# Second feed-forward of a diffusion layer: pools that wait tile by tile, block sums taken from the split parts, and the first output projection moved between the products of one block

## The chip, the cores and the metric

One core of a Trainium2 chip runs the whole program. The metric is device time in microseconds (us) of one execution. A core has a matrix engine (TensorE, PE in the profile; its weight loads are PEld), VectorE (DVE), ScalarE (ACT), GpSimd (POOL) and SyncE (SP), which here issues nearly all DMAs. [...]

## The reference, cut to what matters

One layer works on 512 latent tokens and 256 context tokens of width 1024. It has a first SwiGLU feed-forward, a mixer, and a second SwiGLU feed-forward on the 512 latent tokens. The change touches the second one alone.

```python
def swiglu(y, w_in, w_out):                 # y: 512 x 1024, w_in: 1024 x 5632, w_out: 2816 x 1024
    a, b = jnp.split(y @ w_in, 2, axis=-1)
    return (jax.nn.silu(a) * b) @ w_out
x = ada_out(x, swiglu(ada_in(x, mod, 2, norm_pre[l, 2]), ffn_w_in[l, 1], ffn_w_out[l, 1]), mod, 2, norm_post[l, 2], 0.5)
```

All of it is float32.

## The kernel before

**Precision by splitting.** Every float32 operand of a large product is split into a high part (a copy into a format that TensorE reads in one pass, made by ACT in `split_hi`, L81) and a low part (source minus high, made by DVE in `split_lo` through `sub_to`, L78). `mm3` (L97 to L99) then makes one product out of three matmuls: high by high, low by high, high by low. `mm3p` (L102) is the same with its order fixed. `split_w` splits a weight tile of 128x1024.

**The second feed-forward** works through 22 blocks f of 128 hidden columns. For f = 0 and 1 it makes the a and b products with the full 2 x 24 matmuls per 256 tokens (`products`, `block`), then `gate` takes silu(a) * b and splits it into gh and gl. For f = 2 to 21 it uses a fast form, `in_fast`: the 512 tokens and the 1024 inputs are cut into 2 x 2 blocks (y11, y12, y21, y22), the two weight tiles too (x11, x12 in `ra`, x21, x22 in `rb`), and by Winograd's scheme seven products (12 matmuls of 256 columns each) stand in for eight. This needs sums of blocks. On the side of the tokens `combine` makes t1 = y12 - y11, t2 = y22 - t1, t3 = y22 - y12 and t4 = y21 - t2 once, each split into parts (its second half, t3 and t4, is the function `rest`). On the side of the weights each f makes s1 = x21 + x22 and s2 = s1 - x11 (tile `s12`), s3 = x11 - x21 and s4 = x12 - s2 (tile `s34`), splits both, and splits x11, x12 (tile x) and x22.

In `combine`, y is first put together again from its stored parts yh and yl (four DVE operations of 128x1024, L295, into the tile `yr`); the differences and the low parts follow.

**Output projection.** The f's go in pairs. After the two blocks of pair i, `out_g` multiplies pair i-1 by its rows of w_out: 4 token tiles x 2 column halves, each 2 x 3 matmuls of 512 columns into a bank `pz`, then DVE copies (pair 0, L410) or adds (the others, L412) the bank to the tile z. `out_g` loads and splits its two w_out tiles itself (L395, tag `wo`).

**Order.** The program is written in one order, but the build re-orders it: for each engine it lays out the instruction that is earliest in the program among those that its own estimate takes as ready, and a tile is only given a buffer when one of its tag is free. L97 to L99 may thus move among each other's products; L102 and other marked instructions stay in place. The second feed-forward starts like this (L1187 to L1221): while the last token tiles go through the mixer's output norm, the products of f = 0 and f = 1 for the first 256 tokens (`f2ps[0]`, `f2ps[1]`) and of f = 0 for the last 256 (`f2ps[2]`) are made in order. Then the mixer's pool `mix` closes and the pool `ffn2` opens on its memory.

```python
        for p in f2ps[:2]:
            f2.gate(*p)
        rest = f2.combine(256)
        f2.gate(*f2ps[2])
        f2.block(1, *b1)
        rest()
        f2.fast = True
        f2.run(lambda f: ((NCTX, NLAT),), started=(0, 1))
```

**Buffers that matter.** `raw`: 5 tiles for loaded weights. `win`: 8 tiles for split weights. `sw` (weight sums s12, s34, and t1, t2 of `combine`, the tile `tf`): 2 tiles. `pa`: 4 banks and `pz`: 2 banks for products. A pool opened on memory that another pool had waits, as a whole, for the last instruction that used that other pool. `mix` holds, at its start, the tile `wx` (half of the weights of f = 0), behind it 16 tiles `h`, and then small ones.

Of the kernel before, what the change touches and what calls it, by code (L numbers as in the profile page):

```python
# [8 lines left out]
F32 = mybir.dt.float32  # L9
F32R = mybir.dt.float32r  # L10
# [33 lines left out]
def tile_layer(ctx: ExitStack, tc: tile.TileContext, x, c, ctxt, c_ctx, w_mod, b_mod, norm_pre, norm_post,  # L44
# [194 lines left out]
    class Ffn:  # L239
        def __init__(self, wi, wo_ap, tiles, c_lo, c_hi):  # L240
            self.wi, self.wo_ap, self.tiles, self.c_lo = wi, wo_ap, tiles, c_lo
            self.ncol = c_hi - c_lo
            self.g, self.w, self.fast = {}, {}, False

        def scope(self, pool, done, filler, junk):
            self.pool, self.done, self.filler, self.junk = pool, done, filler, junk
# [37 lines left out]
        def block(self, f, c0, n):  # L284
            self.gate(f, c0, n, self.products(f, c0, n))

        def combine(self, n):


            self.n, c1, c2 = n, self.c_lo, self.c_lo + n  # L290
            k1, k2, cs1, cs2 = slice(0, 4), slice(4, 8), slice(c1, c1 + n), slice(c2, c2 + n)
            y = self.pool.tile([P, KD, 2 * n], F32, tag="z", name="yr", bufs=1)
            for k in (k1, k2):
                for i, cs in enumerate((cs1, cs2)):
                    V.tensor_tensor(out=y[:, k, i * n:(i + 1) * n], in0=yh[:, k, cs].bitcast(F32),  # L295
                                    in1=yl[:, k, cs].bitcast(F32), op=ALU.add)
            y11, y12, y21, y22 = (y[:, k, i * n:(i + 1) * n] for k in (k1, k2) for i in range(2))

            def full():
                return self.pool.tile([P, 4, n], F32, tag="sw", name="tf", bufs=2)  # L300

            t1, t2 = full(), full()
            sub_to(V, t1, y12, y11)
            sub_to(V, t2, y22, t1)
            part_of = iter(self.room(n))

            def split(src):
                hi, lo = next(part_of)
                split_hi(src, hi)
                split_lo(src, hi, lo)  # L310
                return hi, lo

            t2s, t1s = split(t2), split(t1)

            def rest():
                sub_to(V, y12, y22, y12)
                sub_to(V, y21, y21, t2)
                t3s, t4s = split(y12), split(y21)
                own = [(yh[:, k, cs], yl[:, k, cs]) for k, cs in ((k1, cs1), (k2, cs1), (k2, cs2))]
                self.moving = dict(y11=own[0], y21=own[1], y22=own[2], t1=t1s, t2=t2s, t3=t3s, t4=t4s)  # L320

            return rest

        def in_fast(self, f):

            n, pool = self.n, self.pool
            ra, rb = self.loads(f)
            x11, x12, x21, x22 = ra[:, 0:512], ra[:, 512:1024], rb[:, 0:512], rb[:, 512:1024]
            s12, s34 = (pool.tile([P, D], F32, tag="sw", name="sw", bufs=2) for _ in range(2))
            s1, s2, s3, s4 = s12[:, 0:512], s12[:, 512:1024], s34[:, 0:512], s34[:, 512:1024]  # L330
            xh, xl = split_w(ra)
            V.tensor_add(s1, x21, x22)
            sub_to(V, s2, s1, x11)
            sh, sl = split_w(s12)
            sub_to(V, s3, x11, x21)
            sub_to(V, s4, x12, s2)
            uh, ul = split_w(s34)
            x22p = part()
            split_hi(x22, x22p[:, 0:512])
            split_lo(x22, x22p[:, 0:512], x22p[:, 512:1024])  # L340
            lo, hi = slice(0, 512), slice(512, 1024)

            def product(q, wh, wl, y, first=True):
                wh, wl, (mh, ml) = kc(wh), kc(wl), self.moving[y]
                for k in range(4):
                    mm3(q[:, 0:n], wh[:, k], wl[:, k], mh[:, k], ml[:, k], first and k == 0, k == 3,
                        skip_group_check=not first)

            def temp(name):
                return pool.tile([P, n], F32, tag=name, name=name, bufs=1)  # L350

            sg = pool.tile([P, 2 * n], F32, tag="s", name="s", bufs=2)
            cb = pool.tile([P, 2 * n], F32, tag="cb", name="cb", bufs=2)
            qa, qb, qc = pa(), pa(), pa()
            product(qa, xh[:, lo], xl[:, lo], "y11")
            p1 = temp("p1")
            S.copy(p1, qa[:, 0:n])  # L357
            product(qb, sh[:, hi], sl[:, hi], "t2")
            u2 = temp("u2")
            V.tensor_add(u2, p1, qb[:, 0:n])  # L360
            product(qc, sh[:, lo], sl[:, lo], "t1")
            p5 = temp("p5")
            S.copy(p5, qc[:, 0:n])
            product(qa, xh[:, hi], xl[:, hi], "y21", False)
            S.activation(out=sg[:, 0:n], in_=qa[:, 0:n], func=AF.Silu)
            qd = pa()
            product(qd, uh[:, lo], ul[:, lo], "t3")
            u3 = temp("u3")
            V.tensor_add(u3, u2, qd[:, 0:n])
            product(qc, uh[:, hi], ul[:, hi], "y22", False)  # L370
            V.tensor_add(u2, u2, qc[:, 0:n])
            S.activation(out=sg[:, n:2 * n], in_=u2, func=AF.Silu)
            V.tensor_add(cb[:, n:2 * n], u3, p5)
            qe = pa()
            product(qe, x22p[:, lo], x22p[:, hi], "t4")
            V.tensor_add(cb[:, 0:n], u3, qe[:, 0:n])
            V.tensor_mul(cb, cb, sg)
            gh, gl = self.g[f] = tuple(pool.tile([P, self.ncol], F32R, tag=n, name=n, bufs=4) for n in ("gh", "gl"))
            S.copy(gh, cb)
            V.tensor_sub(gl, cb, gh.bitcast(F32))  # L380

        def in_f(self, f, blocks):
            if self.fast:
                return self.in_fast(f)
            if f not in self.w:
                self.weights(f)
            for c0, n in blocks:
                self.block(f, c0, n)
            self.filler()

        def out_g(self, fs, first, last):
            ws = []
            for f in fs:
                r = raw()
                load(r, self.wo_ap[f * P:(f + 1) * P, :])  # L395
                ws.append(split_w(r, pool=self.pool, tag="wo") if len(ws) < 3 else split_w(r))
            z, backs = self.z, Backs(4)
            for i, t in enumerate(self.tiles):
                halves = small(2)
                for h in range(2):  # L400
                    q = pa() if last and i % 2 else pz()
                    cols = slice(h * 512, (h + 1) * 512)
                    for j, f in enumerate(fs):
                        gh, gl = self.g[f]
                        wh, wl = ws[j]
                        ts = slice(t * P - self.c_lo, (t + 1) * P - self.c_lo)
                        (mm3p if last else mm3)(q, gh[:, ts], gl[:, ts], wh[:, cols], wl[:, cols], j == 0,
                                                j == len(fs) - 1)
                    if first:
                        V.tensor_copy(z[:, i, cols], q)  # L410
                    else:
                        add = V.tensor_add(z[:, i, cols], z[:, i, cols], q)  # L412
                        if last and i == len(self.tiles) - 1:
                            tc.keep_in_program_order(add)
                    if last:
                        square_to(halves[:, h:h + 1], z[:, i, cols], self.junk[:, cols])
                        backs.tick()
# [4 lines left out]
        def run(self, blocks_of, started=()):  # L422
            groups = [list(range(2 * i, 2 * i + 2)) for i in range(NF // 2 - 2)] + [list(range(NF - 4, NF))]
            for i, gr in enumerate(groups):
                for f in gr[:2]:
                    if f not in started:
                        self.in_f(f, blocks_of(f))
                if i == 0:
                    self.z = self.pool.tile([P, len(self.tiles), D], F32, tag="z", name="z", bufs=1)
                else:  # L430
                    self.out_g(groups[i - 1], i == 1, False)
                for f in gr[2:]:
                    self.in_f(f, blocks_of(f))
# [759 lines left out]


    with ExitStack() as sx:
        pool = sx.enter_context(tc.tile_pool(name="ffn2", bufs=6))
        junk = pool.tile([P, D], BF16, name="junk3", bufs=1)
        gc2 = pool.tile([P, D], F32, name="gc2", bufs=1)
        bc_row(gc2, (8, 0))
# [5 lines left out]

        f2.scope(pool, done2, lambda: None, junk)

        def room(n):
            th, tl = (pool.tile([P, 2, 4, n], F32R, name=x, bufs=1) for x in ("th", "tl"))
            return [(th[:, 0], tl[:, 0]), (th[:, 1], tl[:, 1])] + [(yh[:, ks, 0:n], yl[:, ks, 0:n])  # L1210
                                                                  for ks in (slice(0, 4), slice(4, 8))]

        f2.room = room
        for p in f2ps[:2]:
            f2.gate(*p)
        rest = f2.combine(256)
        f2.gate(*f2ps[2])
        f2.block(1, *b1)
        rest()
        f2.fast = True  # L1220
        f2.run(lambda f: ((NCTX, NLAT),), started=(0, 1))  # L1221
# [47 lines left out]
```

## Time and profile before

| | us |
|---|---|
| median of 3 runs (1197.02 to 1197.18) | 1197.06 |
| the profiled execution | 1195.69 |
| its span, first to last instruction | 1193.9 |
| PE busy | 1144.2 (96%) |
| DVE busy | 806.5 (68%) |
| ACT busy | 450.8 (38%) |
| POOL busy | 109.2 (9%) |
| mean granted TensorE clock | 0.988 |

The span is 1.8 us shorter than the profiled execution, which is 1.4 us shorter than the median. Times in the rows count from the start of the span. A matmul's shown duration overlaps the next one's; what one costs in a stream is the distance between two starts. The same holds, less so, for the other engines.

### The profile page before, as it was taken

Reading aid. Unit: us, or ns where it says so; the run is one execution under the profiler, and the core shown is the slowest. Engines: PE = TensorE matmul, PEld = TensorE weight load, DVE = VectorE, ACT = ScalarE, POOL = GpSimd, SP = SyncE. Lnnn points to the kernel's source line nnn. Section 1 sums busy time; section 2 is a strip of 40 time slices with the busy share of each in tenths; the row PEclk is TensorE's granted clock in tenths of the full one; section 3 lists DMA queues with packets and bytes.
Section 4 is the critical chain, followed back from the end, with each engine's and each line's share of the span. In section 5 each row is a group of like instructions: output and inputs, shape, how many; then the busy total and the mean of one; then the engine's idle time right before and its main releaser. Section 6 shows DMA issues by size and latency. Waiting matters only on the chain.

```text
span 1193.9 us, 17233 instructions
## 1 busy us (share of the span) xinstructions
PE 1144.2 (96%) x6838; PEld 1041.5 (87%) x6838; DVE 806.5 (68%) x1193; ACT 450.8 (38%) x800; POOL 109.2 (9%) x139
## 2 busy tenths in 40 slices
PE   3999999999999999999999799999799999999996
PEld 2899989899898998989889687888699999999995
DVE  4694967737547343342665877875799888888865
ACT  4532122122121212212494466457544444444431
POOL 4000000000000000000221414412000000000001
PEclk9999999999999999999999899999999999999998
DMA  9955254634435215202223112134144333333321
GB/s 299 299 170 188 93 179 132 199 130 153 165 105 199 80 54 185 69 23 72 88 89 87 56 52 73 63 111 149 59 140 126 106 107 107 106 107 98 99 87 70
DMA packets 140572, 142.48 MB, mean 119 GB/s; under 512 B 6070, under 2 KB 118710, under 8 KB 140492
## 3 DMA queue, kind: packets, MB, share of 16 engines
q1 hardware_dynamic: 140444, 141.38, 37.6%
q8 instruction: 53, 0.87, 0.3%
q14 instruction: 27, 0.22, 0.1%
q10 hardware_dynamic: 48, 0.01, 0.0%
HBM read 135.04 MB, written 6.33 MB: 118 GB/s over the span
## 4 chain that ended last, share of the span: by engine, by line
PE 79%; DVE 6%; ACT 4%; issue 3%; POOL 3%; DMA 1%; SPq 0%; ACTq 0%; POOLq 0%; DVEq 0%
PE pa L99 15%; PE pa L98 15%; PE pa L97 15%; PE pz L97 7%; PE pz L99 7%; PE pz L98 7%; PE pa L102 6%; PE pz L102 4%; PE pt L102 2%; ACT junk L148 2%; POOL sm L143 1%; DVE z L179 1%; PE pt L105 1%; POOL sm L159 1%; DMA raw<-in_w_mod_dram 1%
## 5 line engine op out<-in xcount | busy, mean ns | idle before, releaser
L97 PE MATMUL pa<-yh,wins 128*128 128x384 f32 (+1 forms) x1072 | 338.8, 316 | 2.1 <-ACT p L357 1.2
L99 PE MATMUL pa<-yl,wins 128*128 128x384 f32 (+1 forms) x1072 | 339.3, 317 | 0.0
L98 PE MATMUL pa<-yh,wins 128*128 128x384 f32 (+1 forms) x1072 | 338.4, 316 | 0.0
L97 PEld LDWEIGHTS pa<-yh,wins 128*128 128x128 f32 x1072 | 202.0, 188 | 4.1 <-ACT p L357 1.7
L98 PEld LDWEIGHTS pa<-yh,wins 128*128 128x128 f32 x1072 | 201.8, 188 | 1.6
L99 PEld LDWEIGHTS pa<-yl,wins 128*128 128x128 f32 x1072 | 201.9, 188 | 0.9
L78 DVE TENSOR_TENSOR wins<-raw,wins 128x1024 fp32r<-128x1024 f32 x109 | 123.8, 1138 | 76.9 <-ACT wins L81 69.7
L81 ACT CAST wins<-raw 128x1024 fp32r<-128x1024 f32 x111 | 107.0, 972 | 144.7 <-PE pa L98 105.4
L412 DVE TENSOR_TENSOR z<-z,pz 128x512 f32<-128x512 f32 x170 | 115.6, 685 | 59.2 <-PE pz L99 54.4
L97 PE MATMUL pz<-wos,gh 128*128 128x512 f32 x360 | 142.0, 395 | 0.0
L98 PE MATMUL pz<-wos,gl 128*128 128x512 f32 x360 | 140.4, 390 | 0.0
L99 PE MATMUL pz<-wos,gh 128*128 128x512 f32 x360 | 140.4, 390 | 0.0
L81 ACT CAST wos<-raw 128x1024 fp32r<-128x1024 f32 x42 | 44.0, 1052 | 224.3 <-PE pz L98 202.8
L643 DVE SCALAR_TENSOR_TENSOR m<-m,sc,m 128x1024 f32<-128x1024 f32 x80 | 100.2, 1279 | 0.2
L102 PE MATMUL pa<-yh,wins 128*128 128x512 f32 (+2 forms) x352 | 96.6, 361 | 0.0
L269 DVE TENSOR_TENSOR s<-s,pa 128x384 f32<-128x384 f32 (+1 forms) x46 | 24.9, 544 | 89.8 <-PE pa L99 89.8
L97 PEld LDWEIGHTS pz<-wos,gh 128*128 128x128 f32 x360 | 67.6, 188 | 17.6 <-issue 4.2
L99 PEld LDWEIGHTS pz<-wos,gh 128*128 128x128 f32 x360 | 67.6, 188 | 14.4
L98 PEld LDWEIGHTS pz<-wos,gl 128*128 128x128 f32 x360 | 67.6, 188 | 12.6
L102 PEld LDWEIGHTS pa<-yh,wins 128*128 128x128 f32 x352 | 61.3, 189 | 9.3 <-issue 2.2
L102 PE MATMUL pa<-yl,wins 128*128 128x512 f32 (+2 forms) x176 | 62.1, 353 | 0.0
L78 DVE TENSOR_TENSOR wos<-raw,wos 128x1024 fp32r<-128x1024 f32 x42 | 51.0, 1219 | 14.2 <-ACT wos L81 14.1
(311 smaller groups left out, 1721.9 us busy)
## 6 DMA issues: line engine op xcount, KB each, us to landing
raw<-in_ffn_w_in_dram SPq DMA_DIRECT2D x87, 512.0 KB
m<-in_w_mod_dram SPq DMA_DIRECT2D x57, 512.0 KB
raw<-in_ffn_w_out_dram SPq DMA_DIRECT2D x44, 512.0 KB
raw<-in_w_in_dram SPq DMA_DIRECT2D x16, 512.0 KB
raw<-in_w_mod_dram SPq DMA_DIRECT2D x11, 512.0 KB
m<-in_x_dram SPq DMA_DIRECT2D x8, 512.0 KB
raw<-in_w_out_dram SPq DMA_DIRECT2D x16, 256.0 KB
raw<-x SPq DMA_DIRECT2D x8, 512.0 KB
```

The lines of the kernel that those rows point to most:

```text
L78: return eng.tensor_tensor(out=out_ap, in0=a, in1=b, op=ALU.subtract)
L81: return S.copy(hi, src)
L97: T.matmul(out_ap, lhsT=wh, rhs=xh, start=first, stop=False, **kw)
L98: T.matmul(out_ap, lhsT=wl, rhs=xh, start=False, stop=False, **kw)
L99: T.matmul(out_ap, lhsT=wh, rhs=xl, start=False, stop=last, **kw)
L102: return tc.keep_in_program_order(T.matmul(*args, **kw))
L105: return tc.keep_in_program_order(T.transpose(**kw))
L143: G.tensor_tensor(out=r, in0=ms, in1=mhalf[:, 0:n], op=ALU.pow)
L148: return S.activation(out=junk, in_=src, func=AF.Square, scale=D ** -0.5, accum_out=ssq)
L269: V.tensor_mul(s[:, 0:n], s[:, 0:n], qb[:, 0:n])
L412: add = V.tensor_add(z[:, i, cols], z[:, i, cols], q)
L643: V.scalar_tensor_tensor(out=accs[st], in0=w, scalar=sc[:, st * KD + k:st * KD + k + 1], in1=accs[st], op0=ALU.mult, op1=ALU.add)
```

## The change

It opens `ffn2`, and a new pool `sums` behind it, with waits by tile: a tile waits for those who used its own stretch of memory. `sums` holds t1's and t2's parts (`th`, `tl`) and three `sw` tiles. `combine` no longer puts y together: a difference is the difference of the high parts plus the difference of the low parts (`less`, three DVE operations) or a high part minus a sum plus the low part (`minus`, two). The loads, the x split, s1, s2 and their split of f = 2 are written ahead of the first gates (`first_sums`). The w_out tiles of pair 0 are loaded and split ahead of `rest`. The products go y11, t1, t2, y21, y22, t3, t4 (before: y11, t2, t1, y21, t3, y22, t4). For f = 2, `out_g` of pair 0 stands between t2 and y21 instead of behind f = 3, and ACT instead of DVE copies its banks to z.

```diff
-        def combine(self, n):
+        def combine(self, n, room, temp, step):
...
-            y = self.pool.tile([P, KD, 2 * n], F32, tag="z", name="yr", bufs=1)
-            for k in (k1, k2):
-                for i, cs in enumerate((cs1, cs2)):
-                    V.tensor_tensor(out=y[:, k, i * n:(i + 1) * n], in0=yh[:, k, cs].bitcast(F32),
-                                    in1=yl[:, k, cs].bitcast(F32), op=ALU.add)
...
-            t1, t2 = full(), full()
-            sub_to(V, t1, y12, y11)
-            sub_to(V, t2, y22, t1)
...
-            t2s, t1s = split(t2), split(t1)
+            def less(k, one, two):
+                d, e = temp(), temp()
+                sub_to(V, d, y(k, *one, yh).bitcast(F32), y(k, *two, yh).bitcast(F32))
+                sub_to(V, e, y(k, *one, yl).bitcast(F32), y(k, *two, yl).bitcast(F32))
+                V.tensor_add(d, d, e)
+                return d
+            def minus(half, cs, k, t, new=temp):
+                d = new()
+                sub_to(V, d, y(k, half, cs, yh).bitcast(F32), t)
+                V.tensor_add(d, d, y(k, half, cs, yl).bitcast(F32))
+                return d
+            t1s, t2s, t3s, t4s = room
+            t2 = {}
+            for k in ks:
+                t1 = less(k, (0, cs2), (0, cs1))
+                split(t1, t1s, k)
+                t2[k.start] = minus(1, cs2, k, t1)
+                split(t2[k.start], t2s, k)
             def rest():
-                sub_to(V, y12, y22, y12)
-                sub_to(V, y21, y21, t2)
-                t3s, t4s = split(y12), split(y21)
+                for k in ks:
+                    split(less(k, (1, cs2), (0, cs2)), t3s, k)
+                    split(minus(1, cs1, k, t2[k.start], lambda: t2[k.start]), t4s, k)
...
+        def first_sums(self, f):
+            ra, rb = self.loads(f)
+            s12 = self.sw()
+            s1, s2 = s12[:, 0:512], s12[:, 512:1024]
+            x = split_w(ra)
+            V.tensor_add(s1, rb[:, 0:512], rb[:, 512:1024])
+            sub_to(V, s2, s1, ra[:, 0:512])
+            return x, split_w(s12), s2, (ra, rb)
-        def in_fast(self, f):
+        def in_fast(self, f, between=lambda: None):
...
+            (xh, xl), (sh, sl), s2, (ra, rb) = self.w.pop(f, None) or self.first_sums(f)
+            s34 = self.sw()
...
+            product(qc, sh[:, lo], sl[:, lo], "t1")
+            p5 = temp("p5")
+            S.copy(p5, qc[:, 0:n])
             product(qb, sh[:, hi], sl[:, hi], "t2")
...
-            product(qc, sh[:, lo], sl[:, lo], "t1")
-            p5 = temp("p5")
-            S.copy(p5, qc[:, 0:n])
+            between()
             product(qa, xh[:, hi], xl[:, hi], "y21", False)
             S.activation(out=sg[:, 0:n], in_=qa[:, 0:n], func=AF.Silu)
+            product(qc, uh[:, hi], ul[:, hi], "y22", False)
+            V.tensor_add(sg[:, n:2 * n], u2, qc[:, 0:n])
+            S.activation(out=sg[:, n:2 * n], in_=sg[:, n:2 * n], func=AF.Silu)
             qd = pa()
             product(qd, uh[:, lo], ul[:, lo], "t3")
...
-            product(qc, uh[:, hi], ul[:, hi], "y22", False)
-            V.tensor_add(u2, u2, qc[:, 0:n])
-            S.activation(out=sg[:, n:2 * n], in_=u2, func=AF.Silu)
...
-                        V.tensor_copy(z[:, i, cols], q)
+                        (S.copy if self.fast else V.tensor_copy)(z[:, i, cols], q)
...
+                inside = [lambda: self.out_g(groups[0], True, False)] if i == 1 and self.fast else []
+                for j, f in enumerate(gr[:2]):
+                    if f not in started:
+                        self.in_f(f, blocks_of(f), *(inside if j == 0 else ()))
+                if i and not inside:
                     self.out_g(groups[i - 1], i == 1, False)
...
-        pool = sx.enter_context(tc.tile_pool(name="ffn2", bufs=6))
+        pool = sx.enter_context(tc.tile_pool(name="ffn2", bufs=6, reuse_waits="tile"))
+        sums = sx.enter_context(tc.tile_pool(name="sums2", bufs=1, reuse_waits="tile"))
...
+        th, tl = (sums.tile([P, 2, 4, 256], F32R, name=x, bufs=1) for x in ("th", "tl"))
+        def sw():
+            return sums.tile([P, D], F32, tag="sw", name="sw", bufs=3)
+        f2.sw = sw
+        f2.w[2] = f2.first_sums(2)
         for p in f2ps[:2]:
             f2.gate(*p)
-        rest = f2.combine(256)
+        rest = f2.combine(256, [(th[:, 0], tl[:, 0]), (th[:, 1], tl[:, 1])] +
+                          [(yh[:, k:k + 4, 0:256], yl[:, k:k + 4, 0:256]) for k in (0, 4)],
+                          lambda: sw().rearrange("p (k c) -> p k c", c=256), 4)
         f2.gate(*f2ps[2])
         f2.block(1, *b1)
+        f2.wo = {f: f2.out_weights(f, f) for f in range(2)}
         rest()
```

The feed-forward of the first stage shares the class but keeps its old path (`self.fast` is false there).

## Rows read from the trace of the kernel before

**Rows 1.** Page, part 2: busy tenths and granted clock in 40 slices of 29.85 us.
```profile
PE   3999999999999999999999799999799999999996
...
PEclk9999999999999999999999899999999999999998
```
**Rows 2.** Stretches: us, busy time of PE, PEld, DVE, ACT, POOL (instructions), clock, DMA.
```profile
836.00:846.00 10.00, 9.97 (x85) 9.76 (x83) 2.52 (x3) 4.64 (x8) 0.00 (x0) 1.00 0.41 115
846.00:857.70 11.70, 10.00 (x76) 9.28 (x76) 11.70 (x16) 5.78 (x11) 0.00 (x0) 1.00 0.12 45
857.70:864.70 7.00, 0.00 (x0) 0.00 (x0) 7.00 (x9) 3.81 (x5) 0.00 (x0) 0.84 0.00 0
864.70:869.30 4.60, 4.17 (x18) 3.88 (x19) 4.51 (x7) 3.31 (x4) 0.00 (x0) 0.50 0.57 163
...
960.00:1000.00 40.00, 40.00 (x295) 38.07 (x294) 34.64 (x53) 18.83 (x29) 0.00 (x0) 1.00 0.37 106
```
**Rows 3.** Timeline of PE, 845 to 865: start, us, what, idle before and its releaser.
```profile
846.44 0.39 PE L97 MATMUL pa<-yh,wins 128*128 128x256 f32 x1 [0.47 <-ACT s L268]
846.66 0.28 PE L98 MATMUL pa<-yh,wins 128*128 128x256 f32 x1
846.78 0.28 PE L99 MATMUL pa<-yl,wins 128*128 128x256 f32 x1
...
853.66 0.39 PE L97 MATMUL pz<-wos,gh 128*128 128x512 f32 x1
853.89 0.40 PE L98 MATMUL pz<-wos,gl 128*128 128x512 f32 x1
...
855.97 0.40 PE L97 MATMUL pa<-yh,wins 128*128 128x256 f32 x1 [1.22 <-ACT p L357]
...
864.72 0.80 PE L97 MATMUL pa<-th,wins 128*128 128x256 f32 x2 [7.05 <-ACT wins L81]
```
**Rows 4.** Waits from 836 to 870: who for whom, total us, times, longest.
```profile
PE pa L97 <- ACT wins L81: 7.5, 2, 7.1
DVE yr L295 <- PE pz L102: 5.6, 1, 5.6
...
ACT wins L81 <- DVE sw L78: 2.6, 2, 2.4
```
**Rows 5.** Timeline of DVE, 839 to 864.
```profile
839.66 0.69 DVE L204 TENSOR_TENSOR yl<-yf,yh 128x512 fp32r<-128x512 f32 x1 [1.09 <-ACT yh L203]
846.00 2.36 DVE L295 TENSOR_TENSOR yr<-yh,yl 128x1024 f32<-128x1024 f32 x2 [5.65 <-PE pz L102]
848.28 0.75 DVE L269 TENSOR_TENSOR s<-s,pa 128x256 f32<-128x256 f32 x2
...
862.91 0.68 DVE L78 TENSOR_TENSOR sw<-sw,raw 128x512 f32<-128x512 f32 x1
863.51 0.68 DVE L78 TENSOR_TENSOR sw<-raw 128x512 f32<-128x512 f32 x1
```
**Rows 6.** Groups by form from 840 to 895: count | busy, mean ns | idle before.
```profile
L81 ACT CAST wins<-sw 128x1024 fp32r<-128x1024 f32 x6 | 6.3, 1048 | 7.4 <-DVE sw L78 7.3
...
L410 DVE COPY z<-pz 128x512 f32<-128x512 f32 x7 | 4.8, 687 | 0.5 <-PE pz L99 0.4
```
**Rows 7.** Timeline of SP's DMA queue, 782 to 925.
```profile
830.73 4.77 SPq L114 DMA_DIRECT2D raw<-in_ffn_w_in_dram  x3
...
846.04 0.34 SPq L224 DMA_DIRECT2D gc<-row  x1
864.82 0.33 SPq L395 DMA_DIRECT2D raw<-in_ffn_w_out_dram  x1
867.13 11.29 SPq L114 DMA_DIRECT2D raw<-in_ffn_w_in_dram  x4
```
**Rows 8.** Timeline of ACT, 864 to 876.
```profile
868.50 1.05 ACT L81 CAST wos<-raw 128x1024 fp32r<-128x1024 f32 x1 [1.16 <-DMA raw<-in_ffn_w_out_dram]
```
**Rows 9.** Groups by form of ACT, whole span.
```profile
L992 ACT COPY h<-pz 128x512 f32<-128x512 f32 x4 | 2.4, 596 | 1.3 <-PE pz L102 1.3
```

More of the change, by code (lines that the diff above doesn't have):

```diff
@@ L242, in __init__ @@
             self.ncol = c_hi - c_lo
-            self.g, self.w, self.fast = {}, {}, False
+            self.g, self.w, self.wo, self.fast = {}, {}, {}, False
         def scope(self, pool, done, filler, junk):
@@ L285, in block, with y, split @@
             self.gate(f, c0, n, self.products(f, c0, n))
-        def combine(self, n):
+        def combine(self, n, room, temp, step):
             self.n, c1, c2 = n, self.c_lo, self.c_lo + n
-            k1, k2, cs1, cs2 = slice(0, 4), slice(4, 8), slice(c1, c1 + n), slice(c2, c2 + n)
-            y = self.pool.tile([P, KD, 2 * n], F32, tag="z", name="yr", bufs=1)
-            for k in (k1, k2):
-                for i, cs in enumerate((cs1, cs2)):
-                    V.tensor_tensor(out=y[:, k, i * n:(i + 1) * n], in0=yh[:, k, cs].bitcast(F32),
-                                    in1=yl[:, k, cs].bitcast(F32), op=ALU.add)
-            y11, y12, y21, y22 = (y[:, k, i * n:(i + 1) * n] for k in (k1, k2) for i in range(2))
-            def full():
-                return self.pool.tile([P, 4, n], F32, tag="sw", name="tf", bufs=2)
-            t1, t2 = full(), full()
-            sub_to(V, t1, y12, y11)
-            sub_to(V, t2, y22, t1)
-            part_of = iter(self.room(n))
-            def split(src):
-                hi, lo = next(part_of)
+            cs1, cs2 = slice(c1, c1 + n), slice(c2, c2 + n)
+            ks = [slice(k, k + step) for k in range(0, 4, step)]
+            def y(k, half, cs, part):
+                return part[:, 4 * half + k.start:4 * half + k.stop, cs]
+            def split(src, dst, k):
+                hi, lo = (d[:, k] for d in dst)
@@ L309, in split @@
                 split_hi(src, hi)
                 split_lo(src, hi, lo)
-                return hi, lo
-            t2s, t1s = split(t2), split(t1)
+            def less(k, one, two):
[9 more added lines that the diff above has]
+                return d
@@ L315, in rest @@
+            t1s, t2s, t3s, t4s = room
[5 more added lines that the diff above has]
+                split(t2[k.start], t2s, k)
             def rest():
-                sub_to(V, y12, y22, y12)
-                sub_to(V, y21, y21, t2)
-                t3s, t4s = split(y12), split(y21)
-                own = [(yh[:, k, cs], yl[:, k, cs]) for k, cs in ((k1, cs1), (k2, cs1), (k2, cs2))]
+                for k in ks:
+                    split(less(k, (1, cs2), (0, cs2)), t3s, k)
+                    split(minus(1, cs1, k, t2[k.start], lambda: t2[k.start]), t4s, k)
+                own = [(yh[:, q:q + 4, cs], yl[:, q:q + 4, cs]) for q, cs in ((0, cs1), (4, cs1), (4, cs2))]
@@ L320, in rest @@
                 self.moving = dict(y11=own[0], y21=own[1], y22=own[2], t1=t1s, t2=t2s, t3=t3s, t4=t4s)
             return rest
-        def in_fast(self, f):
-            n, pool = self.n, self.pool
[L327 to L336, printed above, removed]
+        def first_sums(self, f):
[6 more added lines that the diff above has]
+            return x, split_w(s12), s2, (ra, rb)
@@ L337, in in_fast @@
+        def in_fast(self, f, between=lambda: None):
+            n, pool = self.n, self.pool
+            (xh, xl), (sh, sl), s2, (ra, rb) = self.w.pop(f, None) or self.first_sums(f)
+            s34 = self.sw()
+            sub_to(V, s34[:, 0:512], ra[:, 0:512], rb[:, 0:512])
+            sub_to(V, s34[:, 512:1024], ra[:, 512:1024], s2)
             uh, ul = split_w(s34)
-            x22p = part()
+            x22, x22p = rb[:, 512:1024], part()
             split_hi(x22, x22p[:, 0:512])
@@ L353, in in_fast @@
             cb = pool.tile([P, 2 * n], F32, tag="cb", name="cb", bufs=2)
-            qa, qb, qc = pa(), pa(), pa()
+            qa, qc, qb = pa(), pa(), pa()
             product(qa, xh[:, lo], xl[:, lo], "y11")
@@ L380, in in_fast, with in_f @@
             V.tensor_sub(gl, cb, gh.bitcast(F32))
-        def in_f(self, f, blocks):
+        def in_f(self, f, blocks, *between):
             if self.fast:
-                return self.in_fast(f)
+                return self.in_fast(f, *between)
             if f not in self.w:
@@ L389, in in_f, with out_weights @@
             self.filler()
+        def out_weights(self, f, i):
+            r = raw()
+            load(r, self.wo_ap[f * P:(f + 1) * P, :])
+            return split_w(r, pool=self.pool, tag="wo") if i < 3 else split_w(r)
         def out_g(self, fs, first, last):
[L392 to L396, printed above, removed]
+            ws = [self.out_weights(f, i) for i, f in enumerate(fs)] if fs[0] not in self.wo else [self.wo[f] for f in fs]
             z, backs = self.z, Backs(4)
@@ L424, in run @@
             for i, gr in enumerate(groups):
-                for f in gr[:2]:
-                    if f not in started:
-                        self.in_f(f, blocks_of(f))
                 if i == 0:
                     self.z = self.pool.tile([P, len(self.tiles), D], F32, tag="z", name="z", bufs=1)
-                else:
+                inside = [lambda: self.out_g(groups[0], True, False)] if i == 1 and self.fast else []
[3 more added lines that the diff above has]
+                if i and not inside:
                     self.out_g(groups[i - 1], i == 1, False)
@@ L1206, in tile_layer @@
         f2.scope(pool, done2, lambda: None, junk)
[L1208 to L1213, printed above, removed]
+        th, tl = (sums.tile([P, 2, 4, 256], F32R, name=x, bufs=1) for x in ("th", "tl"))
[3 more added lines that the diff above has]
+        f2.w[2] = f2.first_sums(2)
         for p in f2ps[:2]:
             f2.gate(*p)
-        rest = f2.combine(256)
+        rest = f2.combine(256, [(th[:, 0], tl[:, 0]), (th[:, 1], tl[:, 1])] +
+                          [(yh[:, k:k + 4, 0:256], yl[:, k:k + 4, 0:256]) for k in (0, 4)],
+                          lambda: sw().rearrange("p (k c) -> p k c", c=256), 4)
         f2.gate(*f2ps[2])
         f2.block(1, *b1)
+        f2.wo = {f: f2.out_weights(f, f) for f in range(2)}
         rest()
```

## Prediction

> **What bounds the kernel now.** I read the page's slices first, to see where TensorE is not full: after the start it dips in two slices, and the second dip, the slice from 835.7 to 865.6, is where the second feed-forward begins [rows 1]. The stretches around it say how much is lost there. [...] Far behind the joint PE is busy for 40.00 of 40.00 us, DVE for 34.64 [rows 2]: there only TensorE's own work counts.
>
> The size of the loss comes from distances between starts: 0.12 us for a matmul of 256 columns, 0.23 us for one of 512 [rows 3]. From 846.0 to 869.3 PE started 94 matmuls [rows 2], 4 of them of 512 columns (two stand in [rows 3]); 90 x 0.12 + 4 x 0.23 = 11.7 us of work in 23.3 us. **11.6 us are lost.** Of these, 0.47, 1.22 and 7.05 us are waits on ACT [rows 3], another 0.4 us is the second of the two waits on the weight casts [rows 4], and the low clock took 4.6 - 18 x 0.12 - 0.4 = 2.0 us [rows 2].
>
> The releasers tell whose fault it is. PE waits for ACT's cast of the weight sums, that cast waits for DVE's `sw` [rows 4], and DVE writes s1 to s4 only at 861 to 864 (s2 and s3 stand in [rows 5]), behind `combine` and `rest`. DVE itself stood idle from 840.35 (839.66 + 0.69) to 846.00 and was let go by PE's last matmul of `f2ps[2]` [rows 5]: the whole new pool waits for the old one. A queue of DVE work that starts 5.65 us late, in the wrong order, is the bound of this joint.
>
> **The change, part by part.** One DVE operation of 128x1024 costs 1.14 us from start to start (two in 846.00 to 848.28), one of 128x512 0.60 us (862.91 to 863.51), one of 256 columns about 0.35 us (two in 0.75) [rows 5].
>
> *Work added and removed.* `combine` with `rest` had 12 operations of 1.14 us (4 to rebuild y, 4 differences, 4 low parts) and now has 14 (10 and 4): DVE + 2.3 us. Eight copies of a bank to z leave DVE, 8 x 0.69 = - 5.5 us [rows 6], and go to ACT, where the nearest row, a copy of the same shape out of the same banks, takes 0.60 us: + 4.8 us [rows 9]; ACT was busy for 5.78 of 11.70 and 3.81 of 7.00 us [rows 2]. Matmuls and loads are the same in number.
>
> *Waits by tile.* By the tile sizes `ffn2` is 74 KB (2 + 4 + 8 + 8 + 4 + 24 + 16 + 4 + 4); under it lie `wx` (12 KB), which PE reads until 846.0, and the 16 `h` tiles (64 KB). `sums` starts at 74 KB: the very end of the last `h`, then small tiles of the mixer, the last of them read by the DVE operation that ends at 840.35 [rows 5]. So s12, t1, t2 can be written from 840.35 on. `gh` and `gc2` lie over `wx` and still wait for 846.0; that holds up only the ends of the three gates and, on SP's queue, the gc2 row, which already stands at 846.04 [rows 7].
>
> *The new order, deadline against delivery.* PE, after 846.0: block 1 (48 x 0.12) to 851.8, y11 to 853.2, t1 to 854.6, t2 to 856.1, `out_g` (48 x 0.23 = 11.0) to 867.1, y21 to 868.6, y22 to 870.0, t3 to 871.5, t4 to 872.9, then f = 3. DVE, from 840.35: s1 and s2 1.2; t1 3 x 1.14, to 845.0; low part of s12, 846.1; of t1, 847.2; t2 with its low part 3.4, to 850.7; three gates 6 x 0.35, to 852.8. t1 is wanted at 853.2, 6 us after its delivery, t2 at 854.6, 1.8 us after. ACT's casts, 1.05 us each [rows 6], run beside DVE's next operation. Then the two w_out splits, 2.3 us, to 855.1, wanted at 856.1; gate of block 1, 0.7, to 855.8. Under the 11 us of `out_g` DVE does s34 (2.3, to 858.1, wanted at 868.6), `rest` (7 x 1.14, to 866.1; t3 wanted at 870.0), x22 (0.6). Only three `sw` tiles exist, s12 and t2 hold two, and `less` in `rest` needs two: s34 must come first, which frees s12; this order costs nothing, since both end before their deadline. f = 3 then needs x and s12 (1.14 + 1.2 + 1.14) plus some 1.4 us of the sums of f = 2: about 871.6, wanted at 874.4. So at every point DVE is ahead, by 1.0 us at the least (the w_out splits). Cover gone, each of these would be paid in full: `out_g`'s 11 us is the cover of `rest`, and what is late next is the w_out split.
>
> *Loads.* Five `raw` tiles: in the row order f = 2 and f = 3 take four, the first w_out tile one, and the second w_out tile goes out only at 864.82 when s4 has freed a buffer [rows 7]. Now both w_out tiles go ahead of f = 3, and the last tile of f = 3 waits for the first w_out split (855 at the latest). A load lands 3.7 us after its issue (864.82 to 868.50) [rows 7, 8]: 858.7, wanted around 867. Hidden. The tiles of f = 4, now issued at 867.13 [rows 7], still go out when x22 is done. SP has nothing else behind these.
>
> *Product order in the other 19 fast blocks.* Same matmuls, same banks; y22 needs s34 as the fifth product, as t3 did. The steady stretch has no PE wait [rows 2] and DVE has 13% spare. I take 0; ends: 0 below, since no idle time of PE is left there to be won, and a wait like the 0.47 us one [rows 3] in each block above, + 8.9 us, taken up as a rival.
>
> *What stays of the 11.6 us.* The first wait of 0.47 us may stay: block 1 needs banks that ACT's Silu of the gates frees, and ACT now has casts there too. For the start of `out_g` with 1.0 us to spare I put 0.4 us. Ends: 0 and, if both DVE margins below 2 us are used up by ACT in between, 0.47 + 1.8 + 1.0 = 3.3. I take 0.9, the nearer to the row. Gaps of this size do not touch the clock: after the wait of 1.22 us it stayed at 1.00 up to 857.7 [rows 2, 3], after 7.05 us it was at 0.50.
>
> **Sum.** 11.6 - 0.9 = 10.7 us less. The profiled execution took 1195.69 us: 1185.0. The median stands 1.4 us above it: **1186.4 us**.
>
> **Rivals.**
>
> *The pool wait does not go* (the change would not do what it says): some tile under `sums` is still held to 846.0. For: nothing in the rows shows which `h` tile is read last. Then DVE does s1 to the low part of t2 from 846.0: 1.2 + 3.4 + 2.3 + 3.4 = 856.3 and the gates 858.4, against 854.6: 3.8 us; the w_out splits 860.7 against 859.9: 0.8. With a clock cost between 0 (as after 1.22 us) and 2.0 (as after 7.05), say 1.0: 11.6 - 0.9 - 5.6 = 5.1 us less, 1192.0.
>
> *ACT's queue becomes the bound.* A copy of a bank to z can stand behind a cast that still waits for DVE; such casts waited up to 2.4 us [rows 4]. PE works 1.4 us on the other `pz` bank (6 x 0.23), so a hold-up costs 1.0 us, for the casts of s34, t3 and t4 some 3.1 us: 1189.5. For: eight copies now sit among these casts. Against: ACT is half idle and DVE would be ahead.
> [...]
>
> *Slower.* In each of the 19 blocks f = 3 to 21 a small new wait: the y22 sum is now written to the gate's tile by DVE, then taken by ACT in place, and the order of banks changes. From 0.57 us per block on it eats the 10.7 us, from 0.70 us on the kernel is slower by over 0.2%. For: DVE is at 87% in the steady stretch; against: PE there has no wait at all now [rows 2] and the deadlines did not move. At 0.75 us: 1186.4 + 14.3 = 1200.7.
>
> **How the numbers follow.** Forecast (1185.4 to 1188.8) 0.64; pool wait stays 0.14; ACT's queue 0.13; slower 0.05; a mishap that returns about all, such as `rest` laid ahead of the w_out splits and more, 0.04. The first three hold 0.91; the range takes the full loss and a little spread below, 1184.9, and reaches to the pool-wait case, 1191.8. Within 0.2% (2.4 us, about what a measurement can tell from no change) 0.04, slower 0.05, faster 0.91.
>
> **What would show it.** Right: DVE's gap from 840.35 to 846.0 filled with `sw` operations; no PE wait above 1 us and no clock below 1.00 from 846 to 875; `pz` matmuls from about 856 to 867; the block f = 4 beginning near 883 to 884. Wrong: DVE's first `sw` operation released by the last `pz` matmul of `f2ps[2]`; PE waits on ACT's copies to z; a PE gap of some tenths in every block later on.

## The result, and the profile after

| | before | after |
|---|---|---|
| median, us | 1197.04 | 1190.3 (1189.47 to 1190.70) |
| ratio, 95% interval | | 0.9947 [0.9930, 0.9964] |
| profiled execution, us | 1195.69 | 1190.70 |
| span, us | 1193.9 | 1189.0 |

Faster by 6.7 us between the medians, 6.3 by the ratio; 1186.4, a gain of 10.7, was forecast. The profiled execution of before lies 1.4 us under its median and that of after 0.4 us above, so the two spans differ by 4.9 only. A later comparison on another chip (E5) gave 0.9957, 5.7 us between the medians.

The slices of the page, against [rows 1]: the slice from 832 to 862 is full now, and the one behind it has a small dip in PE. The digits of the clock are too coarse to show one.

```profile
PE   4999999999999999999999799999989999999996
...
PEclk9999999999999999999999899999999999999998
```

The stretches, to be laid beside [rows 2] (us, busy time of PE, PEld, DVE, ACT, POOL with instructions, clock, DMA). PE is full up to 857.7, where it was busy for 10.00 of 11.70 us before, and nearly full through the stretch in which it had stood still for 7.00 us. The new hole is behind it, from 869.3 on: 12.02 of 15.20 us at a clock of 0.89.

```profile
836.00:846.00 10.00, 10.00 (x87) 10.00 (x86) 7.01 (x10) 7.31 (x12) 0.00 (x0) 1.00 0.36 108
846.00:857.70 11.70, 11.70 (x95) 11.44 (x94) 11.44 (x15) 5.94 (x12) 0.00 (x0) 1.00 0.27 89
857.70:864.70 7.00, 6.55 (x34) 5.27 (x33) 3.47 (x4) 2.58 (x6) 0.00 (x0) 1.00 0.27 78
864.70:869.30 4.60, 4.50 (x20) 3.38 (x18) 3.83 (x4) 2.45 (x5) 0.00 (x0) 1.00 0.00 0
869.30:884.50 15.20, 12.02 (x83) 11.53 (x84) 14.11 (x21) 9.04 (x13) 0.00 (x0) 0.89 0.41 111
960.00:1000.00 40.00, 40.00 (x295) 38.09 (x294) 35.31 (x54) 19.51 (x29) 0.00 (x0) 1.00 0.34 101
```

The timeline of PE names what it waits for there (start, us, what, idle before and its releaser): 0.45 us for a bank of `pz`, then 2.47 us for ACT's part and 0.79 us for DVE's part of a split weight tile. That tile is s34 of f = 2, which y22 needs. Soon after, the starts lie 0.21 us apart instead of 0.12.

```profile
860.73 0.50 PE L97 MATMUL pz<-wos,gh 128*128 128x512 f32 x1 [0.45 <-ACT z L426]
...
868.82 0.39 PE L99 MATMUL pz<-wos,gh 128*128 128x512 f32 x1
871.68 0.91 PE L97 MATMUL pa<-yh,wins 128*128 128x256 f32 x3 [2.47 <-ACT wins L81]
873.37 0.39 PE L98 MATMUL pa<-yh,wins 128*128 128x256 f32 x1 [0.79 <-DVE wins L78]
...
875.10 0.41 PE L98 MATMUL pa<-yh,wins 128*128 128x256 f32 x1
875.31 0.41 PE L99 MATMUL pa<-yl,wins 128*128 128x256 f32 x1
```

From 874.46 to 877.84 there are 16 such distances, 3.38 us in place of 16 x 0.12 = 1.92: 1.5 us lost to the low clock. **What stays of the joint's loss is 0.45 + 2.47 + 0.79 + 1.5 = 5.2 us.** The prediction put 0.9 there, 4.3 less. Its 10.7 less these 4.3 is 6.4, near the 6.7 and 5.7 measured. The two traces, counted from the same DVE instruction ahead of the joint (839.66 before, 839.82 after) to the end, give 5.1; where the other 1.3 us lie is not shown.

Where s34's lateness comes from stands in DVE's timeline:

```profile
839.82 0.69 DVE L204 TENSOR_TENSOR yl<-yf,yh 128x512 fp32r<-128x512 f32 x1 [1.11 <-ACT yh L203]
840.42 0.68 DVE L340 TENSOR_TENSOR sw<-raw 128x512 f32<-128x512 f32 x1
841.03 1.22 DVE L78 TENSOR_TENSOR sw<-yh 128x1024 f32<-128x1024 f32 x1
...
854.65 1.23 DVE L78 TENSOR_TENSOR tl<-sw,th 128x1024 fp32r<-128x1024 f32 x1
...
856.12 1.22 DVE L78 TENSOR_TENSOR wos<-raw,wos 128x1024 fp32r<-128x1024 f32 x1
857.26 1.22 DVE L78 TENSOR_TENSOR sw<-yh 128x1024 f32<-128x1024 f32 x1
858.39 1.22 DVE L78 TENSOR_TENSOR sw<-yh,sw 128x1024 f32<-128x1024 f32 x1
...
859.96 1.22 DVE L314 TENSOR_TENSOR sw<-sw,yl 128x1024 f32<-128x1024 f32 x1
865.37 1.23 DVE L78 TENSOR_TENSOR yl<-sw,yh 128x1024 fp32r<-128x1024 f32 x1 [4.19 <-ACT yh L81]
866.63 1.23 DVE L78 TENSOR_TENSOR sw<-yl 128x1024 f32<-128x1024 f32 x1
867.89 1.22 DVE L308 TENSOR_TENSOR sw<-sw 128x1024 f32<-128x1024 f32 x1
869.15 0.69 DVE L78 TENSOR_TENSOR sw<-raw 128x512 f32<-128x512 f32 x1
869.76 0.68 DVE L78 TENSOR_TENSOR sw<-raw,sw 128x512 f32<-128x512 f32 x1
```

The late start is gone: 840.42 instead of 846.00 [rows 5]. But behind the w_out splits the order is not the one that I wrote down. The first half of t3's `less` (857.26) takes the one free `sw` tile; its second half would need another. So the build goes on with t4, which is made in place in t2's tile (858.39, 859.96), and t4's low part then waits 4.19 us for its cast. Only that low part's end frees t2's tile for the second half of t3 (866.63), only the sum at 867.89 frees a tile for s34, and s3 and s4 are written at 869.15 and 869.76, last of all.

Why the cast is late stands in ACT's timeline. t4's sum ends at 861.18 (859.96 + 1.22); its cast starts at 864.28, behind four copies of `pz` to z, which wait for PE one after the other:

```profile
860.10 1.07 ACT L426 COPY z<-pz 128x512 f32<-128x512 f32 x2 [2.38 <-PE pz L99]
862.42 0.59 ACT L426 COPY z<-pz 128x512 f32<-128x512 f32 x1 [1.25 <-PE pz L99]
863.80 0.59 ACT L426 COPY z<-pz 128x512 f32<-128x512 f32 x1 [0.80 <-PE pz L99]
864.28 1.05 ACT L81 CAST yh<-sw 128x1024 fp32r<-128x1024 f32 x1
```

### The profile page after: what moved, and what is told of

The parts are those of the page before. It is cut to its first block, busy times and chain, and to the rows that moved or that the text cites. A ratio compares the mean times of both kernels' runs of the same rounds, so it can differ in the third digit from the quotient of the medians.

```text
span 1189.0 us, 17210 instructions
## 1 busy us (share of the span) xinstructions
PE 1145.3 (96%) x6838; PEld 1043.1 (88%) x6838; DVE 804.0 (68%) x1187; ACT 456.1 (38%) x808; POOL 109.3 (9%) x139
## 4 chain that ended last, share of the span: by engine, by line
PE 78%; DVE 7%; ACT 4%; issue 4%; POOL 3%; DMA 1%; SPq 0%; ACTq 0%; POOLq 0%; DVEq 0%
PE pa L99 15%; PE pa L98 15%; PE pa L97 15%; PE pz L97 7%; PE pa L102 7%; PE pz L98 6%; PE pz L99 6%; PE pz L102 4%; PE pt L102 2%; ACT junk L148 2%; DVE wins L78 1%; POOL sm L143 1%; DVE z L179 1%; PE pt L105 1%; POOL sm L159 1%
```

## The experiments

Two theories of the missing 4.3 us. **A, ACT's queue:** the cast of t4 stands behind copies that wait for PE; without them DVE would not have idled, and s34 would have come 4 us earlier. **B, the tiles:** three `sw` tiles, in the order as written, put s34 behind all of `rest`; if s34 is written first, it is in time, wherever the copies are. Ratios are those to the kernel before (1195.66, 1195.76 and 1196.25 us on the three chips).

**E1: the copies to z on DVE again.**

```diff
-                        (S.copy if self.fast else V.tensor_copy)(z[:, i, cols], q)
+                        V.tensor_copy(z[:, i, cols], q)
```


> Pair 0's banks are copied to z by DVE again; all else as changed (1190.3 us). Theory A (held cast: the high part of t4 stands on ACT behind four copies to z that wait for TensorE, and DVE idles 4.2 us for it): DVE's gap of 4.2 us goes, but 8 x 0.69 = 5.5 us of copies come back to DVE, so 1189 to 1191 us. Theory B (missing buffer: only the lack of a fourth sum tile, which puts s34 behind t4, makes TensorE wait at 869; who copies is all one): DVE's order stays, s34 comes no earlier and 5.5 us of DVE work is added ahead of it, 1191 to 1195 us.

1189.21 us, 0.9952 [0.9940, 0.9965]: as the changed kernel (0.9957 in E5). DVE's idle time is gone, but another wait has taken its place. The waits of PE:

```profile
PE pz L97 <- DVE z L426: 4.7, 3, 1.8
```

The copies now stand in DVE's queue among the operations of `rest`, and PE waits for its banks. A's link is real: DVE no longer idles, s3 is written at 865.43 instead of 869.15, and no matmul waits for s34. But taking it away like this frees nothing, since PE now loses 4.7 us on the banks.

**E2: t3's second temporary in a tile of the tag `wo`** (a fourth place for sums; `sums` itself has no room for one).

```diff
-            def less(k, one, two):
-                d, e = temp(), temp()
+            def less(k, one, two, second=temp):
+                d, e = temp(), second()
...
-                    split(less(k, (1, cs2), (0, cs2)), t3s, k)
+                    split(less(k, (1, cs2), (0, cs2), lambda: kc(self.pool.tile([P, D], F32, tag="wo", name="we"), n)), t3s, k)
```


> The second temporary of t3 gets a tile of its own (from the w_out tag, which has two idle at that time), so that t3 no longer waits for the buffer of t4. Theory B (missing buffer): s34's sums move ahead by two DVE operations and one hold-up, the TensorE wait of 2.5 + 0.8 us with its low clock goes, 1185.5 to 1187.5 us. Theory A (held cast): the casts of t3 and t4 still stand behind copies to z, DVE idles about 4 us again and s34 is as late as now, 1189 to 1190.5 us.

1187.24 us, 0.9933 [0.9921, 0.9946]. t3 is no longer torn in two, and DVE's hold-up is 2.0 us. s3 is still written only at 868.75, behind both splits of `rest`. The waits of PE:

```profile
PE pa L97 <- ACT wins L81: 1.6, 1, 1.6
PE pa L98 <- DVE wins L78: 0.5, 1, 0.5
PE pz L97 <- ACT z L426: 0.4, 1, 0.4
```

1.6 + 0.5 instead of 2.47 + 0.79, and from 869.3 to 884.5 the clock is 1.00. About half of the way: the missing tile is part of it; s34's place in the order is what is left.

**E3: s34 of f = 2 written right behind s1 and s2.** Nothing else.

```diff
             sub_to(V, s2, s1, ra[:, 0:512])
-            return x, split_w(s12), s2, (ra, rb)
+            if f != 2:
+                return x, split_w(s12), s2, (ra, rb)
+            s34 = self.s34 = self.sw()
+            sub_to(V, s34[:, 0:512], ra[:, 0:512], rb[:, 0:512])
+            sub_to(V, s34[:, 512:1024], ra[:, 512:1024], s2)
+            return x, split_w(s12), s2, (ra, rb)
...
-            s34 = self.sw()
-            sub_to(V, s34[:, 0:512], ra[:, 0:512], rb[:, 0:512])
-            sub_to(V, s34[:, 512:1024], ra[:, 512:1024], s2)
+            s34 = self.s34 if f == 2 else self.sw()
+            if f != 2:
+                sub_to(V, s34[:, 0:512], ra[:, 0:512], rb[:, 0:512])
+                sub_to(V, s34[:, 512:1024], ra[:, 512:1024], s2)
```


> The sums s3 and s4 of f = 2 are written right behind s1 and s2, ahead of t1. Theory B (missing buffer): s12 is free before rest begins, so rest has its two tiles, nothing waits for t4, y22 has its weights in time: 1185.5 to 1187.5 us. Theory A (held cast): the split of t3 and t4 is still held on ACT by copies to z, t3 instead of y22 is then late at 870 by 1 to 3 us: 1187.5 to 1190 us.

**1184.78 us, 0.9910 [0.9896, 0.9923]: 10.9 us less than before**, the best of all kernels here. The one wait of PE from 830 to 960, and the two stretches in which the changed kernel had lost its time:

```profile
PE pa L97 <- ACT p L377: 0.3, 1, 0.3
```
```profile
857.70:864.70 7.00, 6.77 (x33) 5.21 (x34) 7.00 (x8) 4.32 (x9) 0.00 (x0) 1.00 0.51 150
864.70:869.30 4.60, 4.60 (x22) 3.78 (x22) 4.60 (x7) 3.95 (x7) 0.00 (x0) 1.00 0.27 75
869.30:884.50 15.20, 14.91 (x122) 14.56 (x121) 14.72 (x24) 8.23 (x14) 0.00 (x0) 1.00 0.26 82
```

DVE's timeline shows the price and the return. With s34 and s12 in two of the three tiles, t1 cannot begin before s12 is split, at 848.85 instead of 841.03; its low part starts at 854.05, and no matmul waits for it. s34 is split at 862.67, while PE is busy with `pz` until 870.19, and DVE does not idle in `rest`:

```profile
841.68 0.69 DVE L78 TENSOR_TENSOR sw<-raw 128x512 f32<-128x512 f32 x1
...
848.85 1.22 DVE L78 TENSOR_TENSOR sw<-yh 128x1024 f32<-128x1024 f32 x1
...
854.05 1.22 DVE L78 TENSOR_TENSOR tl<-sw,th 128x1024 fp32r<-128x1024 f32 x1
...
862.67 1.22 DVE L78 TENSOR_TENSOR wins<-sw,wins 128x1024 fp32r<-128x1024 f32 x1
```

B holds: one edit of the order, with the copies left on ACT, brings back all of the missing part. The hold on t4's cast is nearly gone here too (the cast starts at 865.47, its sum ends at 865.02), so E3 does not show what a held cast would cost with s34 first.

**E4: the changed kernel, both pools waiting as a whole; E5: the changed kernel once more.** E4's edit takes `reuse_waits="tile"` from `ffn2` and `sums2`.

> Both pools wait as a whole again, all else as changed. If the earlier start of DVE (840.4 instead of 846.0) carries the gain, as the prediction had it: DVE's chain is 4 to 5.6 us later, TensorE runs out at t1 or t2, 1192 to 1195 us. If the new order alone carries it (out_g and y21 as cover): within 1 us of the changed kernel, 1189.5 to 1191 us.

> The changed kernel itself, on the chip and in the rounds of the next three, so that they can be set against it: ratio to the kernel before 0.993 to 0.9965, with the TensorE waits of 2.5 and 0.8 us behind out_g again.

E4: 1192.6 us, 0.9975 [0.9965, 0.9986]; E5: 1190.08 us, 0.9957 [0.9944, 0.9969]. (Their chips differ, so the ratios are compared.) In E4 the old wait is back:

```profile
DVE sw L340 <- PE pz L102: 5.7, 1, 5.7
```

All the same, the tile wait is worth only 0.0018 of 1196 us, 2 us, here, with intervals that overlap a little: in both kernels s34 comes late, with PE waits of 2.5 and 0.8 us on it.

**E6: E3 with E4's edit.** 

> s3 and s4 early as in the run e3_s34_first (10.8 us under the kernel before), but both pools wait as a whole. If the early start of DVE is needed for the full gain, as the prediction's deadlines say (t2 would come 3 to 4 us late): 4 to 6 us slower than e3_s34_first, ratio to the kernel before 0.9945 to 0.9960. If TensorE finds other work meanwhile (y21 and first parts of out_g stood ahead of t2 already in the changed kernel): at most 2 us slower, ratio 0.9910 to 0.9927.

1188.14 us, 0.9938 [0.9926, 0.9950], between the two ranges expected: with s34 first the tile wait is worth 0.0028, 3.4 us. Of DVE's 5.7 us, PE sees 1.7 us of waits on t1's and t2's casts and 0.5 us on the gates.

**E7: E3 with `out_g` of pair 0 behind f = 3 in the program again; E11: the same edit in the changed kernel.**

```diff
-                inside = [lambda: self.out_g(groups[0], True, False)] if i == 1 and self.fast else []
+                inside = [lambda: self.out_g(groups[0], True, False)] if i == 1 and False else []
```


> As e3_s34_first, but out_g of pair 0 is written behind f = 3 again. If its 11 us are the cover of rest, as the prediction says: TensorE waits for t3 and t4 some 5 to 8 us, ratio 0.9945 to 0.9985. If the build lays parts of out_g there by itself, since nothing else is ready: ratio 0.9905 to 0.9930.

> The changed kernel with out_g of pair 0 written behind f = 3 again (w_out still split early, copies still on ACT). The run e7 showed 0.0004 of difference for this where s34 comes first. If parts of out_g are laid there by the build in any case: ratio 0.9940 to 0.9965, as the changed kernel. If it is needed as cover where s34 is late: 0.9970 to 1.0000.

E7: 1185.26 us, 0.9914 [0.9901, 0.9928], beside E3's 0.9910. E11: 1190.55 us, 0.9951 [0.9939, 0.9964], beside E5's 0.9957, with the same waits of 2.5, 0.8 and 0.4 us. Where `out_g` is written is worth nothing that can be measured: its matmuls are among those that the build may lay out of order, and it puts most of them (39 of 48 up to 868.0 in E7) between the products of f = 2 by itself.

**E8: E3 with the products in the old order** (y11, t2, t1, y21, t3, y22, t4).

> As e3_s34_first, but all fast blocks have the products in the old order y11, t2, t1, y21, t3, y22, t4. If the order is worth nothing in the 19 later blocks and little in f = 2 (the prediction took 0): within 1 us of e3_s34_first, ratio 0.9900 to 0.9922. If t2 ahead of t1 brings the wait for t2's split back: 1 to 3 us more, ratio 0.992 to 0.9935.

1186.06 us, 0.9922 [0.9908, 0.9935], beside 0.9910. The one wait of PE from 830 to 960 is now on t2's cast, since the old order asks for t2 first:

```profile
PE pa L97 <- ACT th L81: 1.4, 1, 1.4
```

The wait agrees with the 1.3 us between the medians. But the intervals overlap, and 0.9922 lies in both of the ranges expected, so a cost of the old order is likely and not shown.

**E9: the changed kernel with the first four copies on DVE and the last four on ACT**, so that no copy stands ahead of t4's cast and half of DVE's burden is gone.

```diff
-                        (S.copy if self.fast else V.tensor_copy)(z[:, i, cols], q)
+                        (S.copy if self.fast and i >= 2 else V.tensor_copy)(z[:, i, cols], q)
```


> The changed kernel with the first four copies of a bank to z on DVE (idle at that time) and the last four on ACT, so that the cast for t4 stands ahead of ACT's copies. Theory A (held cast): DVE's 4.2 us of idle time become 2.4 us of copies and no hold-up, s34 comes 2 to 4 us earlier, TensorE's waits of 2.5 and 0.8 us and the low clock go: ratio to the kernel before 0.9915 to 0.9935 (changed kernel beside it: 0.9957). Theory B (missing buffer alone): s34 still stands behind t4 and the second part of t3, ratio 0.9945 to 0.9965.

1192.06 us, 0.9967 [0.9955, 0.9980]: no gain, and more likely a loss beside E5, though the intervals overlap. The waits of PE, and the stretches:

```profile
PE pz L97 <- DVE z L426: 3.4, 2, 1.8
PE pz L97 <- ACT z L426: 0.7, 1, 0.7
```
```profile
857.70:869.30 11.60, 7.53 (x32) 5.20 (x31) 11.51 (x15) 2.97 (x4) 0.00 (x0) 0.88 0.16 45
```

DVE is busy for 11.51 of 11.60 us, and the four copies wait their turn there. As in E1, DVE has no room for copies in `rest`; and as in E1, s3 comes early (865.81) and no matmul waits for s34. Other than in E1, the clock falls.

**E10: the kernel before with waits by tile on `ffn2`, nothing else.** 

> The kernel before with nothing but the wait by tile on its pool. If the late start of DVE was the bound of the joint, as the prediction read it: DVE starts up to 5.65 us earlier, TensorE's wait of 7.05 us shrinks by 3 to 5.6 us and with it the stretch at the low clock: ratio 0.9940 to 0.9975. If its tiles lie on memory that is read until 846.0: no change, 0.9985 to 1.0010.

1193.64 us, 0.9977 [0.9967, 0.9987], 2.6 us less. DVE's wait shrinks by half only, since `yr`, in z's place, still waits for a matmul that reads what lay under it; PE's large wait stays (it was 7.5 us [rows 4]). What is gone are PE's waits of 1.22 and 0.47 us:

```profile
PE pa L97 <- ACT wins L81: 7.3, 2, 6.9
DVE yr L295 <- PE pz L102: 2.8, 1, 2.8
```

**E12: E3 with E1's edit.** 

> As e3_s34_first, but all eight copies to z on DVE. DVE there has no idle time from 857 to 870; 5.5 us of copies more, less what ACT's queue gives back: TensorE waits 3 to 5 us on copies, ratio 0.9940 to 0.9960. If DVE has room (the prediction counted 2 us ahead of f = 3's s12): 0.9905 to 0.9930.

1194.05 us, 0.9980 [0.9971, 0.9989]: most of E3's gain is lost, more than either range expected. The first copy is laid behind the whole of `rest`; DVE's timeline, the large waits of PE and the stretches:

```profile
868.42 1.22 DVE L78 TENSOR_TENSOR yl<-sw,yh 128x1024 fp32r<-128x1024 f32 x1
869.55 1.28 DVE L432 COPY z<-pz 128x512 f32<-128x512 f32 x2
```
```profile
PE pa L97 <- ACT yh L81: 2.4, 1, 2.4
PE pa L98 <- DVE wins L78: 2.2, 1, 2.2
```
```profile
857.70:869.30 11.60, 6.88 (x34) 5.95 (x34) 11.60 (x13) 4.29 (x7) 0.00 (x0) 0.74 0.46 136
869.30:884.50 15.20, 15.20 (x80) 13.37 (x80) 14.11 (x23) 4.57 (x6) 0.00 (x0) 0.87 0.13 36
```

PE is busy for 6.88 of 11.60 us, and the clock is low in both stretches. The large waits are not on the banks themselves: no `pz` matmul starts between 860.4 and 870.5, since both banks are full until the copies, so there is no output projection left to cover the waits for s34 and for a cast of `rest`. ACT's copies are worth 8.4 us (0.0070) when s34 is first, and nothing when it is last (E1 beside E5).

## Why the prediction came out as it did

The time is in the range by luck. The forecast's own band, 1185.4 to 1188.8, missed it by 1.5 us. The range reaches to 1191.8 for the sake of the pool-wait case, and that case did not come: DVE starts at 840.42. Of the signs named, the filled gap of DVE came. "No PE wait above 1 us and no clock below 1.00" did not (2.47 us, 0.54), and a wait of PE on ACT's copies, named as a sign of being wrong, did, with 0.45 us.

Right, and shown:

- *The place and the size.* The joint was the bound, and what was forecast to be had there is 10.7 us: E3, which changes one order more, takes 10.9.
- *The tile wait does what it says.* DVE's gap from 840.35 to 846.0 is filled from 840.42 on. The rival "the pool wait does not go" put 5.6 us on the opposite; E6 beside E3 shows 3.4. PE's waits on t1 and t2 were 1.7 us there instead of 3.8.
- *ACT's copy* takes 0.59 us; 0.60 was forecast.
- *No new wait in the later blocks.* From 960 to 1000 PE is busy for 40.00 of 40.00 us; behind 960 there is one PE wait, of 0.2 us, which the kernel before has too. The rival with 0.57 us a block is dead.
- *The loads are hidden*: the last tile of f = 3 goes out at 854.61, where 855 was said, and no wait from 836 to 884 is on a DMA.

Wrong:

- **The step that failed is "s34 must come first, which frees s12; this order costs nothing"**, and with it the term "What stays", 0.9 us, which measured 5.2. I had seen the shortage, three tiles of which `less` needs two, and drew from it the order that would be best. The build draws from it the order that is next in the program and can get a tile: half of t3, then t4 in t2's own tile, then the other half, then s34. E3, which writes s34 down ahead of `rest` (and ahead of t1 as well, earlier than I had assumed), comes to about the time that I had predicted. Of the 5.2 us, 1.5 are the low clock, which the prediction had left out for waits of this size.
- *"`out_g`'s 11 us is the cover of `rest`."* The cover is there, but moving `out_g` did not make it (E7, E11).
- *The order of products at 0.* At f = 2 it is likely worth about 1.3 us, by t1 being asked for before t2, but E8's interval does not exclude 0; in the later blocks nothing showed.
- *t2 at 850.7.* Its low part came at 854.65 to 855.88, and PE still did not wait: the build laid y21 and `pz` matmuls ahead of most of t2's product (from 858.24). The margin of 1.8 us was counted from the end of the gates (852.8); from 850.7 it would be 3.9. What saved it was the order of PE's work, laid out when the program was built.

The rival *ACT's queue becomes the bound* gave 1189.5, nearer to the result than my forecast, with the mechanism mirrored: I had copies waiting behind casts; what happened is a cast waiting behind copies. The cast did not pass the copies: ACT stood idle for 1.25 and 0.80 us ahead of two of them while the cast's input was ready (861.18), and the cast started behind them, at 864.28, 3.1 us later.

A and B are links of one chain: the held cast holds t4's tile, the tile holds t3's second half, that holds s34. E3 takes s34 out of it. E1 and E9 cut the first link: s3 comes 3.7 and 3.3 us earlier, and no matmul waits for s34. But PE runs later there, since the copies on DVE cost as much as they free. Whether cutting only the first link would do, with the copies on neither queue's critical part, stays open: no such kernel was tried.

The parts do not add up. Tile waits alone give 2.6 us (E10), in the changed kernel about 2, with s34 first 3.4; ACT's copies 0 or 8.4. Each removes one obstacle on the way to the same products, and what it pays depends on which others are left.

## What to carry to other kernels

Where a build lays out instructions by readiness, a shortage of buffers is an instruction about order: for each tile that is asked for, go through who holds the tag at that moment and which work, later in the program, can go on without one. The order that one would choose has to be written into the program, at best by giving the tile to the urgent user first. And before a chain of copies is moved to an idle engine, look not only at its share but at what urgent short work will stand behind the copies while they wait (here t4's cast, 3.1 us).

## What was not expected of the hardware

The clock fell after two short waits. In the kernel before, a wait of 1.22 us left it at 1.00 [rows 2, 3]; in the changed kernel, PE waits of 2.47 us and, after three matmuls, 0.79 us were followed by 1.00 up to 874.3 and then by 0.54, with most starts 0.21 us apart instead of 0.12 (stretches of the changed kernel):

```profile
872.00:874.30 2.30, 1.50 (x10) 1.12 (x9) 2.30 (x4) 1.09 (x2) 0.00 (x0) 1.00 0.68 202
874.30:878.00 3.70, 3.70 (x21) 3.70 (x20) 2.69 (x5) 1.47 (x2) 0.00 (x0) 0.54 0.50 142
```

So here the low clock came when PE was already busy again (3.70 of 3.70 us). In E2, waits of 1.6 and 0.5 us at the same place left it at 1.00, and the kernel was 2.9 us faster than E5 by the ratios; 1.2 us of waits and the 1.5 us of the clock make 2.7 of them.

The length of the waits does not settle it. In E1 and in E9 PE waits 1.56 and then 1.84 us for a bank, with 12 matmuls of 512 columns between. In E9 the starts behind the second wait go from 0.23 to 0.43 us apart at 866.5, and the clock of the stretch is 0.88. In E1 a third wait of 1.27 us follows, and the clock stays at 1.00:

```profile
857.70:869.30 11.60, 6.94 (x31) 4.88 (x30) 11.52 (x15) 3.51 (x4) 0.00 (x0) 1.00 0.15 43
```

Nor were E1's five executions alike: three took 1188.7 to 1189.2 us at a mean clock of 0.991 or 0.992, two took 1191.3 us at 0.989. What decides whether waits of this size cost the clock stays open.
